# Two-block diffusion and language layer stack on one core: the spatial gate's bias moved from one-row matmuls to a VectorE addition, its product with gelu(u) moved to GpSimd

## The chip, the cores and the metric

One core of a Trainium2 chip runs the whole program. The metric is the device time of one execution in microseconds; the figure to beat is the median of the runs of the kernel before, 2892.49 us. Engines are called TensorE (PE in the rows, its weight loads PEld), VectorE (DVE), ScalarE (ACT), GpSimd (POOL) and SyncE (SP, which here only issues transfers).

## The reference, cut to what matters

The input passes through a first block of two layers (512 tokens of x and 256 tokens of a context, 1024 features, four branches of 256 features each) and then through a second block of two layers with a scan, attention and feed-forward parts. The change touches one branch of the first block only, the spatial gate:

```python
def _spatial_gate(u, v, w_sp, b_sp):
    b, n = u.shape[:2]
    nch = n // CHUNK
    u = jax.nn.gelu(u, approximate=False).reshape(b, nch, CHUNK, SGU_GROUPS, GROUP_W)
    v = jax.nn.gelu(v, approximate=False).reshape(b, nch, CHUNK, SGU_GROUPS, GROUP_W)
    sp = jnp.einsum('gpq,bmqgc->bmpgc', w_sp, v) + b_sp.T[None, None, :, :, None]
    return (u * sp).reshape(b, n, BRANCH_W)
```

CHUNK is 128, there are 4 groups of 64 features. For each chunk of 128 tokens and each group, the tokens of gelu(v) are mixed by a 128 x 128 matrix, a bias per position in the chunk is added, and the result is multiplied by gelu(u). The first layer does it for x (4 chunks) and for the context (2 chunks), the second layer for x alone. The result o_c is the fourth of the branches, and goes on, gated by silu(z), to the merge.

## The kernel before, in words

The program is one straight run of instructions. `layer` (line 569) is called for l = 0 and l = 1; l = 0 is "full" (both streams), l = 1 has x alone. All large products are in float32r with operands split into a high and a low part: `mm3` (line 236) issues three matmuls, high x high (L237), and the two mixed ones (L238, L239). `fm` (line 241) runs them over 8 tiles of features with the weights stationary, 512 (x) or 256 (context) tokens moving. `wload` (line 218) brings 1 MB of weights by one transfer of SyncE's queue into `wraw`, ScalarE casts each half to `whi` (L232), and the low part `wlo` is a subtraction (L233), the first half of the feature tiles on VectorE, the second on GpSimd. There are two buffers of each.

The stretch around the change, in program order: the gate's matrices and its bias are loaded by GpSimd's queue (L610, L612), the matrices are transposed (L615, L617); heads of the first attention branch are made (`proj_heads`), and those of the second beside what follows, piece by piece (`beside`): norms and rotations that pass between ScalarE, VectorE and GpSimd (L966 to L997). Then come the products for v (weights `wcv`, gelu at L640, token-major into `v`), the products for u (weights `wcu`, gelu at L648, feature-major into `u`), the gate itself (L651 to L662), and the Fourier branch, whose products (L679) use a third set of weights, `wbf`, loaded at L673; ScalarE copies them out (L680). Transforms over channels and tokens (L688 to L728) and the attention (`attn1`) follow.

In the gate, for each of two feature tiles j and each stream i, a bank `ps` of PSUM collects, for every chunk m and half h (64 features), an ordinary float32 product of `v` (stationary, 128 rows x 64 columns) with the transposed matrix (moving, 128 columns), and on top of it a product of a row of ones with the row of the bias (one row x 64 columns, 128 moving). VectorE multiplies the full bank by gelu(u) into the branch's tile Y(3, j) in SBUF (L661). A float32 matmul is issued as two instructions on TensorE.

A scheduler in the tile framework orders the instructions of every engine by readiness and priority from its own model and places all waits; the Fourier branch's loads (L670, L672), for instance, stand in the code behind the gate and ran long before it. On the engines, order is then fixed. `urgent` gives the weights' casts and subtractions priority between L632 and L674. After the gate `warm` (L732), a ScalarE instruction that has the exponential's table loaded, reads one element of the last Y(3, 1).

Of the kernel before, what the change touches and what calls it, by code (L numbers as in the profile page):

```python
# [27 lines left out]
# columns of the constant array cst (128 rows)  # L28
# [68 lines left out]
class Kern:  # L97
# [23 lines left out]
    def mt(self):  # L121
        """a bank for products, from the standing ones and those that the phase has lent"""
        self.turn += 1
        pool, tag = self.banks[self.turn % len(self.banks)]
        return self.tl(pool, [P, 512], F32, tag)
# [19 lines left out]
    # ---------------------------------------------------------------- set-up  # L145
# [27 lines left out]
    def setup1(self):  # L173
        """what the first normalisation does not need"""
        nc, I = self.nc, self.I
        nc.gpsimd.dma_start(self.cst[:, P:], I["cst"][:, P:CST_KEEP])
        mk = self.mk = self.tl(self.vp, [P, 2, P], F32, "mk")
        nc.gpsimd.dma_start(mk, I["cst"][:, CST_KEEP:].rearrange("p (a b) -> p a b", a=2))
        self.sink = self.tl(self.cp, [1, 8], F32, "sink")
        nc.gpsimd.dma_start(self.sink, I["sink_d"].rearrange("a b -> (a b)").unsqueeze(0))  # L180
        for gi in (1, 2):
            self.vec_load(gi, nc.gpsimd)
# [34 lines left out]
    # ---------------------------------------------------------------- helpers  # L217
# [23 lines left out]
    def fm(self, ps, w, c0, act, n, m=P, first=True, last=True):  # L241
        """feature-major: ps[m, n] (+)= W[:, c0:c0+m]^T act"""
# [5 lines left out]
    def tm(self, ps, w, c0, n, act, t0, m=P, first=True, last=True):  # L248
        """token-major: ps[m tokens, n] (+)= act^T W[:, c0:c0+n]"""
# [5 lines left out]
    def split(self, hi, lo, src, n=None, eng=None):  # L255
        """hi + lo = src exactly (hi, lo f32r)"""
# [3 lines left out]
    def rsq(self, src, scale, eps, shape, tag="rsq"):  # L260
        """1/sqrt(src*scale + eps) on a small tile"""
# [14 lines left out]
    def stats_fm(self, ssq, n, dim, tag="nrm"):  # L276
        """ssq: squares [128, n] summed over the feature tiles -> r [128, n/128] (token on the partition)"""
# [6 lines left out]
    def add_sq(self, pool, ssq, src, k, tag="sq", bufs=2):  # L284
        """ssq (+)= src^2, tile k of eight; the last added on the vector engine"""
# [14 lines left out]
    def norm_fm(self, tp, xs, n, ssq, w, bias, hi_tag, lo_tag, pool):  # L300
        """xs: 8 feature tiles [128, n], ssq: their squares summed; h = xs*r*w + bias, as hi, lo pairs. In three steps:
        the sums, the factors, the tiles"""
# [16 lines left out]
    # a norm whose factor 1/rms per token is applied after the products: the tiles are scaled by the weight and split as  # L319
    # they are finished  # L320
# [12 lines left out]
    def norm_units(self):  # L333
        """runs evacuations one unit late; the norm's factors follow behind the first and the second unit"""
# [15 lines left out]
    # ---------------------------------------------------------------- first block  # L350
    def silu_c(self):
        """columns silu(c), silu(c_ctx), padded with zeros to 32 columns per k tile"""
# [15 lines left out]
    def ada(self, l, parts):  # L368
        """nb[l][i] = (norm_w*(1+sc), sh, gt) as columns [128, 8] for i = x, ctx: the first two in part 0, the last in
        part 1; yields after every piece"""  # L370
# [5 lines left out]
        def load(m):  # L376
            """two pieces of 1024 columns: of one row tile in part 0, of two in part 1"""
# [50 lines left out]
    def layer0_norm(self, i, hcp):  # L428
        """token-major rms of x or ctx, then, in two halves of the features, feature-major f32"""
# [20 lines left out]
    def ada0(self, h, pool):  # L450
        """the first layer's norm_w*(1+sc) and sh for feature tiles 4h..4h+3; yields after every row tile"""
# [19 lines left out]
        # even and odd row tiles go to column groups of their own  # L471
# [26 lines left out]
    def proj_kv0(self, ada, st, hcp):  # L498
        """the first layer's inputs, and the keys and values of both attention branches, token-major; the second half of
        the features follows the first, so that the products start on half of the modulation"""  # L500
# [68 lines left out]
    def layer(self, l, bst, hcp):  # L569
# [36 lines left out]
        # ---- attention A: heads; SGU and fourier branches beside it  # L606
# [4 lines left out]
        bsp = self.tl(p1, [1, 512], F32, "bsp")  # L611
        nc.gpsimd.dma_start(bsp, I["b_sp"][l].rearrange("g p -> (g p)").unsqueeze(0))  # L612
# [18 lines left out]
        # ---- spatial gate and fourier branches  # L631
# [18 lines left out]
        # spatial gate  # L650
        for j in range(2):  # L651
            for i in streams:
                ps = self.mt()
                for m in range(NS[i] // P):
                    for h in range(2):
# [3 lines left out]
                                 start=True, stop=False)  # L659
                        T.matmul(o, self.ones[0:1, 0:64], bsp[0:1, g * P:(g + 1) * P], start=False, stop=True)  # L660
                V.tensor_tensor(Y(3, j)[i][0], ps[:, :NS[i]], u[i][j], ALU.mult)  # L661
                beside(2)  # L662
        # fourier mix
# [30 lines left out]
        # outputs n and N - n share their cosine and sine sums  # L694
# [35 lines left out]
        # has the exponential's table loaded ahead of the first softmax  # L730
# [6 lines left out]
        # ---- the two attentions  # L737
# [4 lines left out]
        def gates(rs, pool, tag, bufs, steps):  # L742
            """gates z of some branches, applied to them in place"""
# [36 lines left out]
        # ---- gates z  # L780
# [28 lines left out]
        # ---- merge  # L809
# [3 lines left out]
        def merged(i, d):  # L813
            """the merged tile d of stream i (four times its value), split for the output projection"""
# [43 lines left out]
        # ---- output projection and residual  # L858
# [54 lines left out]
    def proj_kv(self, l, st, gc, gx):  # L913
        """finishes the inputs of both streams; keys and values of both attention branches, token-major"""
# [27 lines left out]
    def proj_heads(self, l, br, acts, full, ap, kv):  # L942
        """q, k, v of one attention branch, token-major, rms-normed and rotated"""
# [18 lines left out]
        for half, src, nh, tts in ((0, q, 4, ntt if full else 4), (1, k, 2, ntt)):  # L962
            # rotation tables times the norm's weight
# [38 lines left out]
    def heads_T(self, br, kv, hds, tr, full, ap):  # L1002
        """feature-major exact splits of one group: q stacked [hi; lo], k twice [hi; hi] and [lo; lo]"""
# [27 lines left out]
    def attn1(self, l, hds, tr, Y, full, ap, at, fills):  # L1031
        """grouped attention over [x 512 | ctx 256] keys; br 0 full, br 1 window with sink. Scores and softmax run two
        head tiles ahead of the transposes, those one ahead of p v"""
# [5 lines left out]
        def scores(m):  # L1039
# [11 lines left out]
            # (psum column, key column, width, masks)  # L1051
# [63 lines left out]
    def normalised(self, out, po, sums, nq, pool, tag, bufs=None):  # L1115
        """out = po / sums, for two heads [64, tokens] one above the other; sums [128, tokens/128, 2]"""
# [11 lines left out]
    def run(self, gen):  # L1128
        """exhausts a generator and returns its value"""
# [6 lines left out]
    def every(self, gen, n):  # L1136
        """a generator that advances gen on every n-th step"""
        for _ in gen:
            for _ in range(n):
                yield  # L1140

    def pipeline(self, n, stages):
        """runs stage(m) for m < n; a stage with lag k and period p runs k steps late, on the last of each p items"""
# [6 lines left out]
class Kern2(Kern):  # L1150
    # ---------------------------------------------------------------- rotary tables
    def sincos(self, pool, ang, shape, sin_out, cos_out, tag):
        """sin and cos of ang (f32, any size up to about 1e6): exact reduction mod pi/2, polynomials"""
# [13 lines left out]
        # m = k mod 4  # L1167
# [15 lines left out]
        # quadrants: k = m >= 2, r = odd  # L1183
# [15 lines left out]
    def exp_acc(self, pool, x, shape, tag):  # L1199
        """x <- exp(x) to float32 accuracy, on the vector engine"""  # L1200
# [38 lines left out]
    def rope_tm(self, pool, x, nh, half, cs, sn, out, tag):  # L1239
        """x [P, 4, nh, 2*half] token-major, overwritten; out (may be x) = rotated"""  # L1240
# [12 lines left out]
    def residual(self, act, w, k0=0, scale=None, feed=None, pool=None):  # L1253
        """x += (act @ w (rows k0*128 on)) [* scale]; feeds the next norm if asked; yields after every tile"""
# [20 lines left out]
    # ---------------------------------------------------------------- even layer  # L1275
# [5 lines left out]
    def causal64(self, sc, qi):  # L1281
        """keys of the second half of the diagonal block are hidden from queries of its first half"""
# [29 lines left out]
    def even(self):  # L1312
# [11 lines left out]
        # ---- differential attention  # L1324
# [6 lines left out]
        def proj(g):  # L1331
            """q, k, v of heads 2g, 2g+1, token-major, rotated; and the first head's tiles"""
# [29 lines left out]
        def head(hd, part):  # L1362
            """feature-major exact splits: q stacked [hi; lo], k twice [hi; hi] and [lo; lo]"""
# [16 lines left out]
        def gates(chunks, pool, tmp, steps):  # L1380
            """gates z of the state space branch: twice silu"""
# [42 lines left out]
        def combine(m):  # L1424
            """e0 - lam*(sum0/sum1)*e1: the difference of the two softmaxes, times sum0"""
# [63 lines left out]
        # ---- state space branch  # L1489
# [28 lines left out]
        # dt  # L1518
# [5 lines left out]
        # z; beside it the splits of the attention branch, which goes through its half of the output projection beside the scan  # L1524
# [30 lines left out]
        def done(t):  # L1555
            """gated tile t (twice its value): squares and weighted split for the gated norm"""
# [26 lines left out]
    def softplus(self, pool, src):  # L1583
        """dt [P, 4, 16] (token on the partition) = softplus(src + dt_bias); also -dt*exp(a_log)"""
# [35 lines left out]
    def ssd(self, mp, m1, xs, bT, cT, dt, z, side, done):  # L1620
        """chunks of 128 tokens; xs, bT, cT hold twice their values; xs becomes twice the gated output"""
# [92 lines left out]
    # ---------------------------------------------------------------- feed-forward  # L1714
    def ffn(self, i, last):
# [44 lines left out]
        def weighted(d, t0, n, sq):  # L1760
            """feature tile d, tokens t0..: squares, and token-major the final norm's input times its weight"""
# [23 lines left out]
        if last:  # L1785
            # the last two feature tiles by halves of the tokens: the first half leaves beside the second's products
# [33 lines left out]
class Kern3(Kern2):  # L1820
    # ---------------------------------------------------------------- S5 matrices (from the weights alone)
    # groups g = g2*16 + o2*8 + q; partition (o2, p); unit u = g2*8 + q; chunks of 8 tokens
    def cmul(self, eng, pool, shape, are, aim, bre, bim, ore, oim, tag, conj=False):
        """(ore + i oim) = (are + i aim)(bre + i bim); with conj: oim is minus the imaginary part, aim is given negated"""
# [25 lines left out]
    def s5_coef(self, pool):  # L1850
# [37 lines left out]
        # f = (a - 1)/lam  # L1888
# [454 lines left out]
```

## Time and profile before

| | |
|---|---|
| median of three runs | 2892.49 us (2885.21, 2892.49, 2893.84) |
| span of the profiled execution, first to last instruction | 2888.1 us |
| TensorE matmuls busy | 2797.2 us, 97% |
| TensorE weight loads busy | 2306.0 us, 80% |
| VectorE / ScalarE / GpSimd busy | 1419.7 / 1001.6 / 891.6 us |
| mean granted TensorE clock | 0.982 of full speed |

The profiled execution's own time is not listed apart from the three runs; its span lies 4.4 us under their median and inside their spread. A matmul's end is modelled and overlaps the start of the next, so the spacing of starts is what one costs in a row; a granted clock of 1.00 is 2.4 GHz, 0.50 is 1.2 GHz.

### The profile page before, as it was taken

Reading aid. Unit: us, or ns where it says so; the run is one execution under the profiler, and the core shown is the slowest. Engines: PE = TensorE matmul, PEld = TensorE weight load, DVE = VectorE, ACT = ScalarE, POOL = GpSimd, SP = SyncE. Lnnn points to the kernel's source line nnn. Section 1 sums busy time; section 2 is a strip of 40 time slices with the busy share of each in tenths; the row PEclk is TensorE's granted clock in tenths of the full one; section 3 lists DMA queues with packets and bytes.
Section 4 is the critical chain, followed back from the end, with each engine's and each line's share of the span. In section 5 each row is a group of like instructions: output and inputs, shape, how many; then the busy total and the mean of one; then the engine's idle time right before and its main releaser. Section 6 shows DMA issues by size and latency. Waiting matters only on the chain.

```text
span 2888.1 us, 40028 instructions
## 1 busy us (share of the span) xinstructions
PE 2797.2 (97%) x16056; PEld 2306.0 (80%) x16056; DVE 1419.7 (49%) x2786; ACT 1001.6 (35%) x1796; POOL 891.6 (31%) x676
## 2 busy tenths in 40 slices
PE   7999999999999999999999989999999997999998
PEld 4966788888897888888988767788888865788887
DVE  5615521112346446544577787655542375655532
ACT  3325532222343552333455342332222342432222
POOL 4400153232233124333322232533332220333332
PEclk9989999999998999999999999999999998999999
DMA  6216222121222113332322221223222214233232
GB/s 241 64 43 198 79 63 74 55 73 52 96 72 69 54 52 110 117 108 88 88 81 67 52 90 43 69 83 107 93 95 95 84 45 81 81 94 108 91 99 84
DMA packets 221102, 247.99 MB, mean 86 GB/s; under 512 B 14191, under 2 KB 205268, under 8 KB 219892
## 3 DMA queue, kind: packets, MB, share of 16 engines
q1 hardware_dynamic: 218788, 240.76, 27.0%
q0 software_dynamic: 2128, 4.67, 0.8%
q8 instruction: 126, 2.06, 0.3%
q14 instruction: 60, 0.49, 0.1%
HBM read 231.28 MB, written 6.78 MB: 82 GB/s over the span
## 4 chain that ended last, share of the span: by engine, by line
PE 41%; DVE 4%; issue 4%; DMA 2%; ACT 1%; POOL 1%; SPq 0%; ACTq 0%; POOLq 0%; DVEq 0%
PE ex L237 7%; PE ex L238 7%; PE ex L239 7%; PE mm L237 5%; PE mm L238 5%; PE mm L239 5%; DVE xs L1512 1%; PE mat L2178 1%; DMA s5T<-dkk 1%; PE sg L1676 1%; DVE wlo L233 0%; PE mpo L2208 0%; DMA dcol<-in_ev_d_skip 0%; PE tp L2195 0%; DMA dk<-dk 0%
## 5 line engine op out<-in xcount | busy, mean ns | idle before, releaser
L233 POOL TENSOR_TENSOR wlo<-wraw,whi 128x1024 fp32r<-128x1024 f32 (+3 forms) x180 | 442.0, 2456 | 901.7 <-ACT whi L232 891.6
L232 ACT CAST whi<-wraw 128x1024 fp32r<-128x1024 f32 (+2 forms) x360 | 352.1, 1007 | 600.8 <-issue 205.6
L233 DVE TENSOR_TENSOR wlo<-wraw,whi 128x1024 fp32r<-128x1024 f32 (+2 forms) x180 | 236.1, 1311 | 386.1 <-ACT whi L232 385.5
L237 PE MATMUL ex<-hhi,whi 128*128 128x512 f32 x1044 | 410.8, 394 | 0.6 <-ACT whi L232 0.6
L239 PE MATMUL ex<-hhi,wlo 128*128 128x512 f32 x1044 | 408.9, 392 | 1.6 <-DVE wlo L233 1.6
L238 PE MATMUL ex<-hlo,whi 128*128 128x512 f32 x1044 | 408.6, 391 | 0.0
L237 PE MATMUL mm<-hhi,whi 128*128 128x512 f32 x708 | 282.2, 399 | 4.0 <-ACT whi L232 3.9
L238 PE MATMUL mm<-hlo,whi 128*128 128x512 f32 x708 | 279.0, 394 | 3.2 <-DVE hlo L329 2.8
L239 PE MATMUL mm<-hhi,wlo 128*128 128x512 f32 x708 | 278.8, 394 | 2.1 <-DVE wlo L233 2.0
L239 PEld LDWEIGHTS ex<-hhi,wlo 128*128 128x128 f32 x1044 | 197.0, 189 | 44.2 <-DVE wlo L233 2.5
L237 PEld LDWEIGHTS ex<-hhi,whi 128*128 128x128 f32 x1044 | 197.2, 189 | 42.1 <-ACT whi L232 1.4
L238 PEld LDWEIGHTS ex<-hlo,whi 128*128 128x128 f32 x1044 | 197.2, 189 | 39.8
L237 PEld LDWEIGHTS mm<-hhi,whi 128*128 128x128 f32 x708 | 134.0, 189 | 34.3 <-ACT whi L232 4.8
L239 PEld LDWEIGHTS mm<-hhi,wlo 128*128 128x128 f32 x708 | 133.8, 189 | 31.9 <-DVE wlo L233 3.4
L238 PEld LDWEIGHTS mm<-hlo,whi 128*128 128x128 f32 x708 | 134.0, 189 | 31.0 <-DVE hlo L329 4.1
L237 PE MATMUL mm<-whi,hhi 128*128 128x256 f32 (+1 forms) x464 | 135.3, 292 | 0.1
L239 PE MATMUL mm<-whi,hlo 128*128 128x256 f32 (+1 forms) x464 | 132.5, 286 | 1.4 <-DVE hlo L329 1.4
L238 PE MATMUL mm<-wlo,hhi 128*128 128x256 f32 (+1 forms) x464 | 132.5, 286 | 0.6 <-DVE wlo L233 0.6
L237 PE MATMUL ex<-fhi,whi 128*128 128x512 f32 (+1 forms) x308 | 111.9, 363 | 0.0
L239 PE MATMUL ex<-fhi,wlo 128*128 128x512 f32 (+1 forms) x308 | 111.6, 362 | 0.0
L238 PE MATMUL ex<-flo,whi 128*128 128x512 f32 (+1 forms) x308 | 111.6, 362 | 0.0
L233 POOL TENSOR_TENSOR wblo<-wbraw,wbhi 128x256 fp32r<-128x256 f32 x32 | 26.9, 839 | 235.2 <-ACT wbhi L232 221.5
(822 smaller groups left out, 6098.0 us busy)
## 6 DMA issues: line engine op xcount, KB each, us to landing
wraw<-in_w_merge SPq DMA_DIRECT2D x32, 1024.0 KB
wraw<-in_ev_w_in SPq DMA_DIRECT2D x22, 1024.0 KB
wraw<-in_ffn_gate SPq DMA_DIRECT2D x22, 1024.0 KB
wraw<-in_ffn_up SPq DMA_DIRECT2D x22, 1024.0 KB
wraw<-in_w_in SPq DMA_DIRECT2D x20, 1024.0 KB
wraw<-in_ffn_down SPq DMA_DIRECT2D x17, 1024.0 KB
wraw<-in_w_ada SPq DMA_DIRECT2D x16, 1024.0 KB
wbraw<-in_w_br SPq DMA_DIRECT2D x32, 256.0 KB
```

The costliest lines, as they stand in the source:

```text
L232: self.S.copy(hi[:, a:b], raw[:, a:b])
L233: e.tensor_tensor(lo[:, a:b], raw[:, a:b], hi[:, a:b].bitcast(F32), ALU.subtract)
L237: self.T.matmul(ps, lh, rh, start=first, stop=False)
L238: self.T.matmul(ps, lh, rl, start=False, stop=False)
L239: self.T.matmul(ps, ll, rh, start=False, stop=last)
L1512: V.scalar_tensor_tensor(o, cv[:, tap:tap + 512], cw[:, tap * 12 + t:tap * 12 + t + 1], o, ALU.mult, ALU.add)
L1676: T.matmul(sg[:, j * P:(j + 1) * P], mk, self.c("uincl"), start=True, stop=True)
L2178: T.matmul(sc[:, :n], qT[:, qi * P:(qi + 1) * P], kT[:, :n], start=True, stop=False)
```

## The change: what it does, and the diff

The bias is loaded as a tile of 128 partitions: row 64h + c holds, for j = 0, 1, the 128 biases of group 2j + h, the same for all 64 c. Two transfers of GpSimd's queue per layer, each repeating 256 numbers into 64 partitions, take the place of one. The one-row matmuls go; each remaining product opens and closes its own sum. VectorE adds the bias as it moves the bank to Y(3, j), reading the bias tile with a repeat over the chunks, and GpSimd multiplies Y(3, j) by gelu(u) in place. Elsewhere the diff only removes comments.

```diff
-        bsp = self.tl(p1, [1, 512], F32, "bsp")
-        nc.gpsimd.dma_start(bsp, I["b_sp"][l].rearrange("g p -> (g p)").unsqueeze(0))
+        bsp = self.tl(p1, [P, 2, P], F32, "bsp")
+        for h in range(2):
+            nc.gpsimd.dma_start(bsp[64 * h:64 * h + 64], I["b_sp"][l].rearrange("(j h) p -> h j p", h=2)[h].unsqueeze(0)
+                                .to_broadcast([64, 2, P]))
...
                         T.matmul(o, v[:, 4 * i + m, g * 64:g * 64 + 64], wspT[:, g * P:(g + 1) * P],
-                                 start=True, stop=False)
-                        T.matmul(o, self.ones[0:1, 0:64], bsp[0:1, g * P:(g + 1) * P], start=False, stop=True)
-                V.tensor_tensor(Y(3, j)[i][0], ps[:, :NS[i]], u[i][j], ALU.mult)
+                                 start=True, stop=True)
+                y = Y(3, j)[i][0]
+                V.tensor_tensor(y.rearrange("p (m q) -> p m q", q=P), ps[:, :NS[i]].rearrange("p (m q) -> p m q", q=P),
+                                bsp[:, j].unsqueeze(1).to_broadcast([P, NS[i] // P, P]), ALU.add)
+                G.tensor_tensor(y, y, u[i][j], ALU.mult)
                 beside(2)
```

## Rows read from the trace of the kernel before

**Rows 1.** The page: its head, and the engines' busy time.

```profile
span 2888.1 us, 40028 instructions
...
PE 2797.2 (97%) x16056; PEld 2306.0 (80%) x16056; DVE 1419.7 (49%) x2786; ACT 1001.6 (35%) x1796; POOL 891.6 (31%) x676
```

**Rows 2.** Instructions of the one-row matmuls' line; duration ns min/median/max, first and last start.

```profile
L660 PE MATMUL ex<-bsp,ones x56: 267/416/471, 148.2 to 921.2; 1*64 1x128 f32 x56
...
L660 PE MATMUL mm<-bsp,ones x24: 416/442/471, 153.9 to 167.7; 1*64 1x128 f32 x24
```

**Rows 3.** Busy us by stretch of layer 0's gate; PEclk is the granted clock.

```profile
147.80:153.90 6.10, 6.10 (x35) 3.20 (x34) 0.18 (x1) 1.67 (x2) 0.00 (x0) 1.00 0.00 0
153.90:173.00 19.10, 19.10 (x63) 8.88 (x62) 1.63 (x3) 0.00 (x0) 0.00 (x0) 0.50 0.00 1
173.00:177.50 4.50, 4.50 (x12) 3.51 (x12) 0.42 (x1) 0.20 (x1) 0.00 (x0) 0.50 0.00 0
```

**Rows 4.** Timeline of TensorE, layer 0, gate and Fourier products: start us, us.

```profile
147.80 0.43 PE L658 MATMUL ex<-wspT,sguv 128*64 128x128 f32 x2
148.16 0.43 PE L660 MATMUL ex<-bsp,ones 1*64 1x128 f32 x2
...
173.03 0.80 PE L237 MATMUL ex<-hhi,whi 128*128 128x512 f32 x1
...
178.09 0.40 PE L237 MATMUL ex<-hhi,whi 128*128 128x512 f32 x1
...
180.85 0.28 PE L237 MATMUL ex<-chi,whi 128*128 128x256 f32 x1
```

**Rows 5.** Timeline of TensorE, layer 1, the Fourier products behind the gate.

```profile
921.55 0.80 PE L237 MATMUL ex<-hhi,whi 128*128 128x512 f32 x1
...
922.57 0.63 PE L239 MATMUL ex<-hhi,wlo 128*128 128x512 f32 x1
...
925.45 0.40 PE L237 MATMUL ex<-hhi,whi 128*128 128x512 f32 x1
```

**Rows 6.** Timeline of TensorE in layer 0's attention.

```profile
236.40 1.53 PE L1107 MATMUL mm<-pt,hkv 128*64 128x128 f32 x24
237.86 0.39 PE L1071 MATMUL at<-tk,tq 128*128 128x256 f32 x1
...
257.43 0.43 PE L1107 MATMUL mm<-pt,hkv 128*64 128x128 f32 x2
257.79 0.44 PE L1093 MATMUL tp<-cst,e 128*128 128x128 f32 x2
```

**Rows 7.** Timeline of ScalarE, VectorE and GpSimd before and beside layer 1's gate.

```profile
907.74 0.38 ACT L640 ACTIVATE sguv<-ex 128x256 f32<-128x256 f32 x1
...
883.82 1.42 DVE L997 TENSOR_TENSOR hq<-hq,hrs 128x256 f32<-128x256 f32 x4
...
907.68 3.58 DVE L997 TENSOR_TENSOR hq<-hq,hrs 128x256 f32<-128x256 f32 x4
...
915.89 1.22 DVE L233 TENSOR_TENSOR wlo<-wraw,whi 128x1024 fp32r<-128x1024 f32 x1
...
919.37 0.68 DVE L661 TENSOR_TENSOR y<-ex,sguu 128x512 f32<-128x512 f32 x1
...
907.91 2.40 POOL L233 TENSOR_TENSOR wlo<-wraw,whi 128x1024 fp32r<-128x1024 f32 x1 [0.47 <-ACT whi L232]
```

**Rows 8.** Timeline of VectorE, ScalarE and GpSimd around layer 0's gate.

```profile
141.24 1.22 DVE L233 TENSOR_TENSOR wlo<-wraw,whi 128x1024 fp32r<-128x1024 f32 x1
...
173.66 0.20 ACT L732 ACTIVATE warm<-xc 1x1 f32<-1x1 f32 x1 [24.08 <-DVE xc L661]
...
198.83 0.60 POOL L702 DMA_DIRECT2D fc<-in_dft  x1 [61.14 <-PE ex L720]
```

**Rows 9.** GpSimd's in-place multiplication of a branch by its gate z.

```profile
L759 POOL TENSOR_TENSOR x<-x,mt x8: 1289/1292/1297, 355.6 to 415.3; 128x512 f32<-128x512 f32 x8
```

**Rows 10.** GpSimd's issue of the bias transfer, both layers.

```profile
L612 POOL DMA_DIRECT2D bsp<-in_b_sp x2: 518/524/530, 79.4 to 825.7; - x2
```

## The prediction, made before the changed kernel ran

> **What bounds the kernel.** I read the page first. TensorE is busy 97% of a span of 2888.1 us, and no other engine passes half [rows 1]: what shortens TensorE's own run of work, and is not given back in a wait, shortens the kernel. Then the one-row matmuls' line: 56 + 24 = 80 instructions [rows 2], which is 40 matmuls, 24 in layer 0 (two feature tiles, six chunks, two halves) and 16 in layer 1, in two instructions each. As many products of v stay. Then the stretches of layer 0's gate by time: TensorE's granted clock is 1.00 (2.4 GHz) for the first 6.1 us, 0.50 (1.2 GHz) for the next 19.1 us, and still 0.50 in 4.5 us of the Fourier products behind it [rows 3]. So the gate takes 25.2 us of TensorE, from 147.80 to 173.03 [rows 4], and slows what follows. Its 96 instructions cost 180 ns each while the clock is full: 0.36 us from the pair of line 658 to the pair of line 660 [rows 4].
>
> The last view settles what the products cost alone. In the attention, line 1107 has the same shape (128 rows, 64 columns, 128 moving, float32, the two column halves taking turns every two instructions). 24 of them in a row take 1.46 us, from 236.40 to 237.86, so 61 ns each; a lone pair between products of another shape takes 0.36 us, from 257.43 to 257.79, again 180 ns each [rows 6]. It is the change of shape every two instructions that is dear, and the one-row matmuls cause it. Removing them removes their time and two thirds of their neighbours'.
>
> **Part 1, TensorE in layer 0.** 48 instructions stay: 48 x 61 ns = 2.9 us, with 0.2 us for coming in from another shape (a lone pair's 0.36 less 2 x 61 ns) 3.1 us, so the Fourier products start at 150.9 and not at 173.03: 22.1 us. Do they find their weights? The last subtraction for them on VectorE ends at 141.24 + 1.22 = 142.5 [rows 8], 8 us before. In that stretch nothing else is late. The clock: the gate had 6.1 us at full clock before it fell [rows 3], and now ends after 3.1, so I take it that it does not fall. Then the first 12 Fourier products, 5.06 us from 173.03 to 178.09, cost what the next 12 do, 2.76 us [rows 4]: 2.3 us more. Layer 0 gives 24.4 us.
>
> **Part 2, TensorE in layer 1.** Here the gate hides something. TensorE would be through the gate early: the last chunk of v is ready at 908.1 [rows 7], and 20 instructions behind it take 1.2 us, so 909.3. But VectorE, which is in a closed run of work for the second heads, subtracts the first half of the Fourier weights only at 915.89, until 917.11 [rows 7]. That instruction waits for nothing of the gate, so it stays there. The third Fourier product, the first to read that half, started at 922.57 [rows 5] and can now start at 917.1: 5.5 us. TensorE comes to it after a pause of 8 us; I let it be at 1.2 GHz for about as long as it was at 921.55, to 925.45 [rows 5], which lasts 0.7 us longer in product time than what remained of it before. I take 4.5 us. From below: if the additions are put ahead of that subtraction on VectorE it is up to 2 x 0.68 us [rows 7] later, and GpSimd's multiplications can hold it up: the same four instructions of line 997 took 3.58 us beside a subtraction of GpSimd (907.91, 2.40 us) and 1.42 us at 883.82 [rows 7], 2.2 us more, about one GpSimd instruction. That leaves 1 to 2 us. From above: with the subtraction early, 921.55 - 909.3 = 12.2 us, and 1.8 us more for the first 9 products at full clock (3.90 us against 9 x 0.23) [rows 4, 5]: 14 us.
>
> On those held-up instructions, the Trainium skill (SBUF — State Buffer, Who interferes with whom) says that a VectorE instruction with two inputs in SBUF and a GpSimd instruction that reads SBUF exclude each other for a whole instruction. The trace agrees (3.58 against 1.42 us); by it layer 1 would give some 2 us instead of 4.5 if both multiplications ran before 917.
>
> **Part 3, the evacuation.** VectorE's instruction stays in number and shape, PSUM and one SBUF operand in; it was 0.68 us for 512 tokens [rows 7]. No row has the repeated bias operand. Between the same 0.68 and twice that, it costs nothing, since the banks of the gate are not the next that the Fourier products take. New on GpSimd are four multiplications in layer 0 and two in layer 1. The in-place one of line 759 takes 1.29 us [rows 9]; all six are under 8 us. In layer 0 GpSimd is idle for 61 us up to 198.83 [rows 8], and nothing queues behind them. In layer 1 its weight subtraction starts at 907.91 [rows 7]; I take the multiplications to come behind it. Who waits for the product? First `warm` on ScalarE, with the copies of the Fourier products behind it. It ran at 173.66, when VectorE had finished [rows 8]; now it waits for GpSimd too: the last products end at 150.9, addition and queued multiplications bring that to 153.5 or so, and the first copy is due when 24 Fourier products are through, 5.5 us after 150.9. Cover: 3 us. If it fails, copies come late, but the transforms that read them stand further behind. Nothing.
>
> **Part 4, the transfers.** One more transfer in each layer on GpSimd's queue, 0.52 us of issue each [rows 10], in front of heads and a weight subtraction. They start some 70 us ahead of the gate. Between 0 and 1 us each, if many more packets are slower to issue; I take 0.5 in all.
>
> **Sum.** 24.4 + 4.5 - 0.5 = 28.4 us. The span would be 2859.7. Against the median, 4.4 us above the span, 2892.5 - 28.4 = **2864 us**. A measurement of this kernel can tell about 0.3%, 8.7 us, from no change.
>
> **Rivals.** (a) *The remaining products stay at 180 ns*, the shape change not being the reason. For it: the gate has only been seen at this price. Against: line 1107 [rows 6]. Layer 0 would be 48 x 180 ns = 8.6 us, or 10.4 if the clock falls again after 6.1 us (34 instructions, then 14 at the 303 ns that 19.1 us for 63 of them give [rows 3]): 14.8 to 16.6 us saved, perhaps 2.3 with the clock. Layer 1 stays at 4.5, bound by 917.1. 19 to 23 us: 2869 to 2873. The Trainium skill (TensorE: Matmul & The Clock Gate, Part 3) has a rule on this side: a weight load overlaps matmuls in flight only when the row group differs, and the products left use all rows. By it they would not overlap; the 61 ns of line 1107, whose row groups do not differ either, speak against it. Chance 0.11.
>
> (b) *VectorE's order frees the weights early in layer 1*: the scheduler, with other times, moves the subtraction up. Then 24.4 + 14 = 38 us: 2854. Against: nothing ahead of it depends on the gate. 0.10.
>
> (c) *The time is given back*: work behind the gate in layer 0 is bound by something that does not move. Against: TensorE is the busy engine there too. Within 8.7 us: 2884 to 2901. 0.05.
>
> (d) *Slower*: the scheduler reorders TensorE's work in the attention, so that its runs of one shape are cut up. Place: line 1107, 61 ns in a long run and 180 ns in a pair [rows 6]. Price: 0.12 us for each instruction that loses its run. It decides when the loss passes the 28 us saved; to be slower by 8.7 us it takes 37 / 0.12 = 308 instructions. For it: the order comes from a model that sees the change. Against: little changes ahead of the attention but a shift in time. With 340 so cut, 2905. 0.03.
>
> **Numbers.** The forecast has 0.71, (a) 0.11, (b) 0.10, (c) 0.05, (d) 0.03. Faster: the first three, 0.92; same 0.05; slower 0.03. The range takes in (a) up to 2873 and (b) down to 2854 with some 3 us for the spread of runs (2885 to 2894): 2851 to 2876.
>
> **What would show it.** Right: line 658 in layer 0 as one run of 48 instructions in about 3 us, the Fourier products at about 151 at a clock of 1.00 from the start; in layer 1 a TensorE pause of 7 to 9 us that ends with VectorE's `wlo`. Wrong: 180 ns between products of line 658 (rival a); no pause in layer 1 (b); new idle time of TensorE between 170 and 300, or shorter runs of line 1107 (c, d).

## The result and the profile after

The changed kernel took 2862.48 us (median of 4 runs, 2858.03 to 2865.51) against 2890.65 us for the kernel before in runs beside it (4 runs, 2885.21 to 2893.84). The ratio is 0.9897, with a 95% interval of 0.9874 to 0.9920: faster by 1.0%, 28.2 us between the medians. In the changed file the product of the gate stands at line 660, VectorE's addition at 663, GpSimd's multiplication at 665; the transforms of 688 and 706 are now 692 and 710, `warm` is 736 and line 997 is 1001.

The page of the changed kernel, its head and the engines' busy time, answers to [rows 1]:

```profile
span 2856.1 us, 39868 instructions
...
PE 2758.6 (97%) x15976; PEld 2287.8 (80%) x15976; DVE 1418.5 (50%) x2786; ACT 1000.1 (35%) x1796; POOL 897.6 (31%) x684
```

The span is 32.0 us shorter. TensorE has 80 instructions less and 38.6 us less busy time, GpSimd eight instructions more (six multiplications and two transfers), VectorE the same number.

TensorE's timeline in layer 0 (start us, us), where the gate is now one run of 16 + 24 + 8 = 48 instructions, to set against [rows 4]:

```profile
148.64 1.09 PE L660 MATMUL ex<-wspT,sguv 128*64 128x128 f32 x16
149.57 1.48 PE L660 MATMUL mm<-wspT,sguv 128*64 128x128 f32 x24
150.88 0.61 PE L660 MATMUL ex<-wspT,sguv 128*64 128x128 f32 x8
151.41 0.50 PE L237 MATMUL ex<-hhi,whi 128*128 128x512 f32 x1
...
154.29 0.39 PE L237 MATMUL ex<-hhi,whi 128*128 128x512 f32 x1
```

The gate goes from 148.64 to 151.41, 2.8 us where it was 25.2. The first 12 Fourier products take 2.88 us, to 154.29, where they took 5.06 [rows 4]. The stretches of time say why (as in [rows 3]; behind the length stand busy us and instructions of PE, PEld, DVE, ACT and POOL, then the granted clock, the share of the DMA engines and GB/s):

```profile
148.60:151.40 2.80, 2.80 (x49) 2.60 (x48) 1.33 (x3) 1.67 (x2) 0.78 (x1) 1.00 0.00 0
151.40:160.00 8.60, 8.60 (x51) 7.60 (x50) 0.72 (x2) 0.79 (x2) 3.14 (x4) 1.00 0.01 2
...
884.80:891.50 6.70, 1.29 (x4) 0.50 (x2) 6.36 (x19) 1.82 (x2) 2.42 (x1) 0.50 0.00 0
```

In layer 0 the granted clock is 1.00 (2.4 GHz) through the gate and behind it. In layer 1 it is 0.50 (1.2 GHz) from 884.8 to 891.5, a stretch in which TensorE is busy for 1.29 of 6.70 us. TensorE's timeline there (the bracket is the idle time before an instruction and what ended it) answers to [rows 5]:

```profile
878.86 0.66 PE L660 MATMUL ex<-wspT,sguv 128*64 128x128 f32 x8
880.37 0.44 PE L660 MATMUL ex<-wspT,sguv 128*64 128x128 f32 x4 [0.85 <-ACT sguv L642]
882.53 2.40 PE L660 MATMUL ex<-wspT,sguv 128*64 128x128 f32 x20 [1.72 <-ACT sguv L642]
884.86 0.80 PE L237 MATMUL ex<-hhi,whi 128*128 128x512 f32 x1
...
891.52 0.79 PE L239 MATMUL ex<-hhi,wlo 128*128 128x512 f32 x1 [5.43 <-DVE wlo L233]
...
904.01 1.00 PE L692 MATMUL tp<-wf,c 128*128 128x64 f32 x8
```

TensorE waits three times: twice for ScalarE's gelu of v inside the gate, then 5.43 us for VectorE's `wlo`. VectorE's timeline shows what that subtraction stands behind, to set against [rows 7]:

```profile
882.04 3.59 DVE L1001 TENSOR_TENSOR hq<-hq,hrs 128x256 f32<-128x256 f32 x4
...
890.25 1.22 DVE L233 TENSOR_TENSOR wlo<-wraw,whi 128x1024 fp32r<-128x1024 f32 x1
...
893.73 1.28 DVE L663 TENSOR_TENSOR y<-ex,bsp 128x512 f32<-128x512 f32 x2
```

The weights' half is ready at 891.5, and the gate's additions come 2.2 us behind it. What follows them on the two other engines:

```profile
894.49 2.53 POOL L665 TENSOR_TENSOR y<-y,sguu 128x512 f32<-128x512 f32 x2 [6.66 <-DVE y L663]
```

```profile
897.05 0.20 ACT L736 ACTIVATE warm<-y 1x1 f32<-1x1 f32 x1 [10.42 <-POOL y L665]
898.77 0.59 ACT L684 COPY fT<-ex 128x512 f32<-128x512 f32 x1 [1.51 <-PE ex L239]
```

`warm` ends 1.5 us before the first copy of the Fourier products is due. So it holds up nothing yet, but little is left.

The gain, from one starting point to the next: layer 0's gate begins 0.84 us later than before (an early wait for the first weights' transfer, 7.4 against 6.6 us, makes most of it); the Fourier products begin 21.6 us sooner (173.03 to 151.41), the transforms behind them 23.8 us sooner (192.01 to 168.18), layer 1's gate 25.6 us sooner (904.50 to 878.86), and its first transforms 30.3 us sooner (934.32 to 904.01).

### The profile page after: what moved, and what is told of

Read it like the earlier page. It is cut to its first block, busy times and chain, and to the rows that moved or that the text cites. A ratio compares the mean times of both kernels' runs of the same rounds, so it can differ in the third digit from the quotient of the medians.

```text
span 2856.1 us, 39868 instructions
## 1 busy us (share of the span) xinstructions
PE 2758.6 (97%) x15976; PEld 2287.8 (80%) x15976; DVE 1418.5 (50%) x2786; ACT 1000.1 (35%) x1796; POOL 897.6 (31%) x684
## 3 DMA queue, kind: packets, MB, share of 16 engines
q1 hardware_dynamic: 218788, 240.76, 27.3%
## 4 chain that ended last, share of the span: by engine, by line
PE 42%; DVE 4%; issue 4%; DMA 2%; ACT 1%; POOL 1%; SPq 0%; ACTq 0%; POOLq 0%; DVEq 0%
PE ex L238 7%; PE ex L237 7%; PE ex L239 7%; PE mm L237 5%; PE mm L238 5%; PE mm L239 5%; DVE xs L1516 1%; PE mat L2182 1%; DMA dk<-dk 1%; PE sg L1680 1%; DMA s5T<-dkk 1%; DVE wlo L233 0%; PE mpo L2212 0%; DMA dcol<-in_ev_d_skip 0%; PE tp L2199 0%
```

## The experiments

In the edits below "before" and "changed" say which kernel is edited. The kernel before took 2889.84 us (13 runs) beside experiments 1 to 4, 2894.73 (11) beside 6, 7, the first run of 8 and 9, and 2894.80 (7) beside 5, the second run of 8 and 10; all ratios are against those. Three dots in an edit or in rows mark a cut.

**1. GpSimd's product alone.** The change's other half without the matmul's: before, with the evacuation split in two.

```diff
-                V.tensor_tensor(Y(3, j)[i][0], ps[:, :NS[i]], u[i][j], ALU.mult)
+                y = Y(3, j)[i][0]
+                V.tensor_copy(y, ps[:, :NS[i]])
+                G.tensor_tensor(y, y, u[i][j], ALU.mult)
```

> The kernel before with its one-row matmuls, VectorE only copying the bank out and GpSimd multiplying by gelu(u): half of the change alone. I expect no difference, span 2888 within 5 us: six GpSimd instructions, under 8 us, in stretches where nothing queues behind them. If the product on GpSimd costs something by itself, it shows here as a later start of the Fourier products or of their copies.

2890.36 us, ratio 1.0004 (0.9992 to 1.0016): no difference that these runs can tell. Its layer 0 gate took 27.0 us, from 149.09 to 176.13.

**2. The product back on VectorE.** Changed, one word.

```diff
-                G.tensor_tensor(y, y, u[i][j], ALU.mult)
+                V.tensor_tensor(y, y, u[i][j], ALU.mult)
```

> The changed kernel with the product with gelu(u) back on VectorE, behind the addition: GpSimd gets nothing new. If the time comes from TensorE alone, as I hold, this is the changed kernel again: span 2856 within 4 us, layer 0's gate 2.8 us, layer 1's pause ended by the same VectorE subtraction. If GpSimd's part matters (a product that holds up the ScalarE instruction behind it, or a VectorE that is too full for both), it differs by over 4 us, to either side.

2858.57 us, ratio 0.9887 (0.9872 to 0.9901), not to be told from the change's. `warm` ran 2.2 us behind the first Fourier product (155.12 and 152.90) where it was 3.2 us behind in the changed kernel, and in layer 1 the third Fourier product waited 5.50 us for VectorE's `wlo`, as with the change. The gain comes from what is done to the one-row matmuls; which engine multiplies makes no difference that these runs can tell.

**3. The same matmuls with 128 rows.** Before, with as many instructions, in the same order on TensorE; the bias is row 0 of a zeroed tile, so the sum is the same.

```diff
-        bsp = self.tl(p1, [1, 512], F32, "bsp")
+        bsp = self.tl(p1, [P, 512], F32, "bsp")
+        G.memset(bsp, 0.0)
...
-                        T.matmul(o, self.ones[0:1, 0:64], bsp[0:1, g * P:(g + 1) * P], start=False, stop=True)
+                        T.matmul(o, self.ones[:, 0:64], bsp[:, g * P:(g + 1) * P], start=False, stop=True)
```

> The kernel before with as many matmuls, but the bias product made in the shape of its neighbours: 128 rows of ones against a tile that holds the bias in row 0 and zeros below. If it is the change of shape that is dear, the 96 instructions of layer 0's gate take 96 x 58 ns = 5.6 us instead of 25.2, the clock stays at 1.00 there, and layer 1 gains the same 4.7 us as the changed kernel, since VectorE's subtraction ends its wait: 22 + 5 - 1 = 26 us, span about 2862. If it is the number of matmuls, the gate stays at about 25 us and the span at 2888.

2859.78 us, ratio 0.9889 (0.9872 to 0.9905). TensorE's timeline:

```profile
148.45 0.45 PE L659 MATMUL ex<-wspT,sguv 128*64 128x128 f32 x4
148.72 0.40 PE L661 MATMUL ex<-bsp,ones 128*64 128x128 f32 x4
...
153.89 0.50 PE L237 MATMUL ex<-hhi,whi 128*128 128x512 f32 x1
```

The 96 instructions take 5.4 us. So it was not their number that cost 25.2 us, but that every second pair had another number of rows.

**4. One-row matmuls, grouped.** Before, with one bias matmul per half and bank ahead of all products of the bank, so that the shape changes twice per bank.

```diff
+                n = NS[i]
+                for h in range(2):
+                    g = 2 * j + h
+                    T.matmul(ps[64 * h:64 * h + 64, :n].rearrange("c (m q) -> c m q", q=P), self.ones[0:1, 0:64],
+                             bsp[0:1, g * P:(g + 1) * P].unsqueeze(1).to_broadcast([1, n // P, P]), start=True, stop=False)
...
-                                 start=True, stop=False)
-                        T.matmul(o, self.ones[0:1, 0:64], bsp[0:1, g * P:(g + 1) * P], start=False, stop=True)
...
+                                 wspT[:, g * P:(g + 1) * P], start=False, stop=(m == n // P - 1))
```

(The 128 biases of a group are read again for each chunk, so 8 one-row matmuls in layer 0 cover the columns that 24 covered before.)

> The kernel before with one-row matmuls kept, but one per half bank, ahead of the products, its bias row repeated over the chunks: 8 one-row matmuls in layer 0 and 4 in layer 1 instead of 24 and 16, and two changes of shape per bank instead of one every two instructions. If the change of shape is dear: per bank of 512 about 4 x 0.22 + 16 x 0.058 + 2 x 0.24 = 2.3 us, of 256 about 1.4, so layer 0's gate 7 to 8 us, span about 2864. If an instruction beside one-row matmuls costs 180 ns wherever it stands, the gate takes about 12 us and falls to half clock.

2863.73 us, ratio 0.9905 (0.9890 to 0.9919). TensorE's timeline:

```profile
147.91 1.07 PE L657 MATMUL ex<-bsp,ones 1*64 1x512 f32 x4
148.91 1.09 PE L662 MATMUL ex<-wspT,sguv 128*64 128x128 f32 x16
...
154.29 0.50 PE L237 MATMUL ex<-hhi,whi 128*128 128x512 f32 x1
```

The gate takes 6.4 us with one-row matmuls in it, over as many columns. What is dear is the alternation, not the one row.

**5. How many rows.** As in 3, with 32 and with 64 rows in place of 128.

```diff
-        bsp = self.tl(p1, [P, 512], F32, "bsp")
+        bsp = self.tl(p1, [64, 512], F32, "bsp")
...
-                        T.matmul(o, self.ones[:, 0:64], bsp[:, g * P:(g + 1) * P], start=False, stop=True)
+                        T.matmul(o, self.ones[0:64, 0:64], bsp[:, g * P:(g + 1) * P], start=False, stop=True)
```

> The kernel before with the bias product on 32 rows (31 of them zero) between products of 128 rows. If any change in the number of rows is dear, this is the kernel before: pairs 0.36 us apart at full clock, layer 0's gate some 25 us, span about 2888. If it is the single row, the gate falls toward the 5.4 us of the version with 128 rows.

> The same with 64 rows. If any change in the number of rows is dear, 25 us and 2888 again; if the cost shrinks as the shapes come closer, between 5.4 and 25 us.

One run each: 2877.93 us with 32 rows, 2872.13 with 64. TensorE's timeline with 64 rows, the first pairs and the last:

```profile
149.00 0.43 PE L659 MATMUL ex<-wspT,sguv 128*64 128x128 f32 x2
149.36 0.43 PE L661 MATMUL ex<-bsp,ones 64*64 64x128 f32 x2
...
165.96 0.43 PE L661 MATMUL ex<-bsp,ones 64*64 64x128 f32 x2
166.32 0.50 PE L237 MATMUL ex<-hhi,whi 128*128 128x512 f32 x1
```

The gate takes 17.3 us, all pairs 0.36 us apart, and the clock stays whole, as the stretch shows:

```profile
149.00:166.30 17.30, 17.30 (x97) 9.09 (x96) 1.81 (x3) 1.67 (x2) 0.00 (x0) 1.00 0.00 1
```

With 32 rows the pairs are 0.36 us apart too until the clock falls, 9.4 us into the gate:

```profile
148.00:157.70 9.70, 9.70 (x57) 5.18 (x55) 1.12 (x2) 1.67 (x2) 0.00 (x0) 1.00 0.01 2
157.70:171.20 13.50, 13.50 (x47) 6.21 (x45) 0.69 (x1) 0.00 (x0) 0.00 (x0) 0.51 0.00 0
```

It takes 22.8 us (148.41 to 171.19). So the price of a pair at full clock is the same with 1, 32 and 64 rows, while the time to the fall of the clock is not. Layer 1's gates, one of each kernel, go the same way: the clock falls 3.6 us in with one row (experiment 6, 879.57 to 883.17), 10.1 us in with 32 (901.99 to 912.07), and not in the 11.6 us with 64.

What happens within a pair is seen in the weight loads. Those of the 64-row kernel:

```profile
149.00 0.19 PEld L659 LDWEIGHTS ex<-wspT,sguv 128*64 128x64 f32 x2
149.36 0.19 PEld L661 LDWEIGHTS ex<-bsp,ones 64*64 64x64 f32 x2 [0.17 <-issue]
149.72 0.19 PEld L659 LDWEIGHTS ex<-wspT,sguv 128*64 128x64 f32 x2 [0.17 <-issue]
```

and those of the 128-row kernel of experiment 3, whose program order is the same:

```profile
148.44 0.20 PEld L659 LDWEIGHTS ex<-wspT,sguv 128*64 128x64 f32 x4
148.61 0.26 PEld L661 LDWEIGHTS ex<-bsp,ones 128*64 128x64 f32 x4
```

With other rows the engine of the loads stands idle for 0.17 us before each pair of them, and nothing that the profile shows holds it. With the same rows four loads go in 0.20 us: the product of the second column half starts about 0.01 us behind that of the first, though the first half's bias matmuls stand ahead of it in the program. (The order that is fixed in the program is thus not the order of starts on TensorE.) The halves run side by side, each a new instruction every 0.11 us (148.61 to 148.72). Equal rows thus give two things: no gap, and two halves at once.

It need not be the rows that differ. The lone pair of [rows 6] in the kernel before has 64 columns between instructions of 128 columns, all with 128 rows, and its loads show the same gap on both sides:

```profile
257.43 0.19 PEld L1107 LDWEIGHTS mm<-pt,hkv 128*64 128x64 f32 x2 [0.17 <-issue]
257.79 0.20 PEld L1093 LDWEIGHTS tp<-cst,e 128*128 128x128 f32 x2 [0.17 <-issue]
```

No experiment varies the columns by themselves.

**6. The change in layer 0 alone.** Changed, with the old gate in layer 1.

```diff
-                                 start=True, stop=True)
+                                 start=True, stop=full)
+                        if not full:
+                            T.matmul(o, self.ones[0:1, 0:64], bs1[0:1, g * P:(g + 1) * P], start=False, stop=True)
                 y = Y(3, j)[i][0]
+                if not full:
+                    V.tensor_tensor(y, ps[:, :NS[i]], u[i][j], ALU.mult)
+                    beside(2)
+                    continue
```

(In layer 1 the bias row `bs1` is loaded by one transfer, and VectorE multiplies at once, as before.)

> The change in layer 0, layer 1's gate as in the kernel before (its one-row matmuls and its product on VectorE). If the two gates add up as their stretches read, layer 0 alone gives 22.5 us for the gate, 2.3 for the clock behind it, so 24 to 26 us against the kernel before, and layer 1's 4 to 5 us are missing against the changed kernel: span about 2861. If layer 1's waits made its gate free, the span is 2856 as changed.

2864.78 us (6 runs), ratio 0.9905 (0.9889 to 0.9921). Layer 1's gate again took 17.2 us, 879.57 to 896.73, though VectorE's `wlo` was ready at 892.1.

**7. The changed kernel again,** beside 6, 8 and 9.

> The changed kernel once more, on the chip of the last three, to compare with: span 2856 within 4 us.

2860.11 us, ratio 0.9887 (0.9869 to 0.9905). The median is 4.7 us below that with layer 0 alone, but the intervals of the two ratios overlap.

**8. The Fourier weights' first half on GpSimd in layer 1.** Changed; the subtraction that TensorE waits for moves to the engine that does the second half. No other instruction of any engine changes its place. Run twice.

```diff
-            for a, b, e in ((0, h, self.V), (h, kt, self.G)):
+            for a, b, e in ((0, h, lo_eng or self.V), (h, kt, self.G)):
...
-        wbf = self.win(l, 1536)
+        wbf = self.win(l, 1536, lo_eng=None if full else G)
```

> The changed kernel with one instruction moved in layer 1: the first half of the Fourier weights' subtraction goes from VectorE to GpSimd, ahead of the second half. If VectorE's place for it is what ends TensorE's pause, the pause of 5.4 us goes: the third Fourier product starts within 1 us of the second, the clock is low for a shorter time, and the Fourier products end some 6 us sooner against the changed kernel. Span about 2850, ratio to the changed kernel 0.998. If something else is late there too, the pause stays at 3 us or more.

> The version with the Fourier weights on GpSimd once more, beside the swap and for a second sample against the changed kernel: 2855 us within 4, ratio 0.987 to 0.989 to the kernel before.

2855.73 us (ratio 0.9879, 0.9860 to 0.9897) and 2857.60 us (0.9874, 0.9856 to 0.9892). TensorE's timeline of the first run:

```profile
882.97 2.40 PE L660 MATMUL ex<-wspT,sguv 128*64 128x128 f32 x20 [1.73 <-ACT sguv L642]
...
886.32 0.63 PE L239 MATMUL ex<-hhi,wlo 128*128 128x512 f32 x1
...
901.42 1.13 PE L710 MATMUL tp<-bd,fT 128*128 128x256 f32 x4 [1.80 <-ACT bd L696]
```

The 5.43 us wait is gone, but the transforms of line 710 now wait 1.80 us for ScalarE, whose timeline has

```profile
898.63 0.20 ACT L736 ACTIVATE warm<-y 1x1 f32<-1x1 f32 x1 [11.57 <-POOL y L665]
...
900.63 0.73 ACT L696 COPY bd<-tp 64x256 f32<-64x256 f32 x2
```

`warm` still waits for GpSimd's product and, through it, for VectorE's addition, and the copies queue behind it. The cover of 1.5 us is used up, and the edit itself takes part of it: `warm` runs 19.3 us behind the gate's start (898.63 - 879.30) where it ran 18.2 us behind (897.05 - 878.86), although VectorE has an instruction of 1.22 us less to do. Its four instructions of line 1001 now stand beside three subtractions of GpSimd and take longer than the 3.59 us above:

```profile
884.61 5.76 DVE L1001 TENSOR_TENSOR hq<-hq,hrs 128x256 f32<-128x256 f32 x4
```

**9. Heads kept out of the gate's gelus.** As 8, and in layer 1 no head work is called between the chunks of v.

```diff
-            beside(1)
+            beside(1 if full else 0)
```

> As the one with the Fourier weights on GpSimd, and in layer 1 no pieces of the second heads are put between the products for v, so that ScalarE's gelus are not queued behind the heads' squares. If these gelus make TensorE wait 0.85 and 1.72 us within the gate, both go: some 2.5 us less again, span about 2848. If the heads come due later because of it, the time comes back in front of the attention and the span is 2850 or more.

2859.58 us, ratio 0.9883 (0.9866 to 0.9901), and TensorE's two waits for the gelus were still 0.85 and 1.73 us. This tested nothing: the scheduler gave every engine the same instructions in the same order as in 8, so the gelus stayed where they were, and these runs are a third sample of 8.

**10. The last gelu ahead of the casts.** As 8, and in layer 1 v's gelu gets a high priority, which puts the last of them ahead of the two weight casts in ScalarE's order and changes nothing else.

```diff
-            S.activation(v[:, tt, :], ps[:, :256], AF.Gelu)
+            with (nullcontext() if full else self.tc.high_priority()): S.activation(v[:, tt, :], ps[:, :256], AF.Gelu)
```

> The version with the Fourier weights on GpSimd, and in layer 1 the last gelu of v ahead of the casts of those weights on ScalarE (one swap). TensorE's pause of 1.7 us within the gate goes, the weights come 0.4 us later; the third Fourier product starts about 1 us sooner after the gate's start. In the total this is under what five rounds can tell: within 0.1% of that version.

2859.62 us, ratio 0.9879 (0.9865 to 0.9894): no gain over 8. TensorE's timeline:

```profile
881.27 1.59 PE L660 MATMUL ex<-wspT,sguv 128*64 128x128 f32 x24 [0.85 <-ACT sguv L642]
...
895.63 1.00 PE L692 MATMUL tp<-wf,c 128*128 128x64 f32 x8
901.91 2.07 PE L710 MATMUL tp<-bd,fT 128*128 128x256 f32 x4 [4.84 <-ACT bd L696]
```

The second wait is gone and the Fourier products end 1.7 us sooner than in the second run of 8 (895.63 and 897.31, both with the gate's start at 879.76), but line 710 starts at the same time (901.91 and 901.90): the wait for ScalarE grew from 3.15 to 4.84 us.

From the start of layer 1's gate to the first instruction of line 710 (706 before, other lines in experiments 5 and 6) the traces give:

| kernel | us |
|---|---|
| before; layer 0 alone (6) | 32.1; 32.0 |
| changed; again (7) | 27.4; 27.3 |
| experiment 8, both runs; 9; 10 | 22.1, 22.1; 22.1; 22.1 |
| experiment 5, 64 rows (line 707) | 25.4 |

All four profiles with the early weights stop at the same 22.1 us; by their waits it is `warm` and the copies behind it that set this. The early weights are thus worth 5.2 us at line 710. Some of it is given back: the instruction of line 1076 that starts 90.4 and 90.0 us behind the gate in the two profiles of the changed kernel starts 86.1 to 86.9 us behind it in these four. In the times it is 3.1 us between means (13 runs of 8 and 9 together 2858.0, eight of the changed kernel 2861.2), where single runs of either spread by 8 to 9 us: a likely small gain, not a shown one. A version in which `warm` reads something that is ready sooner was not tried.

The last row of the table shows a second price of the waits. With 64 rows, layer 1's gate takes 11.6 us, not 6.0, but TensorE has almost no wait in it or behind it, and the clock stays whole:

```profile
894.00:905.60 11.60, 11.60 (x65) 6.06 (x64) 10.70 (x32) 6.88 (x10) 6.79 (x8) 1.00 0.00 1
905.60:915.00 9.40, 9.06 (x40) 7.17 (x39) 4.59 (x10) 0.79 (x2) 0.00 (x0) 1.00 0.66 224
```

The third Fourier product, held by VectorE's `wlo`, comes 12.6 us behind the gate's start there and 12.7 us in the changed kernel; from it to the end of the Fourier products it is 10.6 us there and 12.5 us here, where the clock is down at first. So this one gate, the slower by itself, ends 2.0 us ahead at the transforms.

## Why the prediction was right

**Size and sign.** The forecast was a gain of 28.4 us; the medians differ by 28.2, the spans by 32.0. The interval of the ratio reaches from 23 to 36 us, so that the two agree within 0.2 us is luck. The two profiles of the same changed kernel have spans of 2856.1 and 2861.6 us and agree within 0.5 us up to 1025 us, so some 5 us of a span are the later part's own spread, and the predicted 2859.7 lies between them. In the profile shown, TensorE's instructions stand 30.4 us sooner from layer 1's transforms to 1480 us of the kernel before; all of that but 1.8 us is in the parts below, less the 0.84 us by which the first gate begins later.

**Part 1, layer 0.** The step from [rows 6] held: 58 ns for each of the 48 instructions (2.77 / 48) where line 1107 gave 61. The gate gave 22.5 us for 22.1, the Fourier products behind it 2.2 for 2.3, the clock not falling. The reason given for the clock, that the gate would be over before the 6.1 us at which it had fallen, was weak: the same gate lost it after 3.6 us in experiment 1, and the 64-row gate kept it for 17.3 us. Rival (a), products that stay at 180 ns, fell with TensorE's timeline of layer 0.

The price of one change of shape was taken as a single number; the experiments take it apart. Of the 25.2 us, by differences between kernels, 7.9 us are the fall of the clock (25.2 less 17.3 with 64 rows), 11.9 us the change of rows at full clock (17.3 less 5.4 with 128 rows), 2.6 us the number of matmuls (5.4 less 2.8), and 2.8 us stay. The 11.9 us can be split by an estimate: 96 instructions at 0.11 us, one half at a time and without gaps, are 10.5 us, so some 5 us come from the halves no longer running side by side and some 7 us from the gaps.

On that, the Trainium skill (TensorE: Matmul & The Clock Gate, Part 3) has the rule weighed in the prediction, that a weight load overlaps matmuls in flight only if its row group differs. The loads of experiment 3 go against it, as line 1107 did: four of them, all with the same 128 rows, go within 0.20 us, the later ones while products are in flight. The 0.17 us of idle time before each pair of loads with other rows, which are among those 128, decides nothing about it.

**Part 2, layer 1.** 4.7 us (32.1 less 27.4 in the table) for 4.5. The medians of experiments 6 and 7 differ by as much, which agrees but, with intervals that overlap, shows nothing by itself. What bounds it was named rightly: VectorE's `wlo`, in its place in the run for the heads. Moved by the 25.6 us that layer 1's gate begins sooner, its steps come out one by one: v's last chunk forecast at 908.1 - 25.6 = 882.5, and those products start at 882.53; the weights' half at 917.1 - 25.6 = 891.5, and the third Fourier product starts at 891.52. The lower clock behind it was to take back 0.7 us: the third product came 5.41 us sooner after the gate's start, of which 4.7 remain. Only the pause was not the 7 to 9 us forecast: the last 20 products took 2.4 us at 1.2 GHz where 1.2 us had been put, and two Fourier products another 1.2 us, which leaves 5.43 us of it. Both lie in the same wait and change no sum.

Rival (b), the weights ready early, did not come by itself; experiment 8 made it happen. The Fourier products end 25.2 us after the gate's start in the changed kernel (904.01 - 878.86), 18.9 and 17.5 us in the two runs of experiment 8, and 15.9 us in experiment 10, where a wait for a gelu is gone as well: 6.3, 7.6 and 9.3 us less, for the rival's 14 - 4.5 = 9.5. What reached line 710 was 5.2 us. The step that failed, in the rival alone, is that nothing would be late next: `warm` is.

**Part 3, the evacuation and GpSimd.** The addition with the repeated bias operand takes 0.68 to 0.69 us for 512 tokens, the lower of the two bounds. The products take 1.28 us, as [rows 9] had for line 759, and cost nothing (experiments 1 and 2). The additions came behind `wlo` and the multiplications behind both, so the feared hold-up did not touch the weights. The cover for `warm` in layer 0 was named rightly: forecast to run at 153.5, it ran at 154.57, and the first copy was due at 157.21.

The four instructions of line 1001 took 3.59 us, beside a subtraction of GpSimd. That is the hold-up of [rows 7] again and agrees with the Trainium skill (SBUF — State Buffer, Who interferes with whom), as weighed in the prediction: 3.59 us beside GpSimd, 1.42 us without [rows 7].

**Part 4.** The second bias transfer doubles GpSimd's issue (0.52 to 1.24 us), and the wait for the gate's weights beside it in layer 0 grew from 0.75 to 0.85 us: 0.1 us where 0.5 was allowed.

**Not forecast.** Between layer 0's transforms (23.8 us sooner) and layer 1's gate (25.6) lie 1.8 us that no part of the change has a price for. In the kernel before the granted clock was down for part of the way, 0.93 in the stretch

```profile
810.00:835.00 25.00, 22.92 (x154) 20.87 (x153) 19.20 (x50) 10.40 (x19) 7.12 (x9) 0.93 0.17 57
```

and the stretch that answers to it in the changed kernel had it whole:

```profile
786.00:811.00 25.00, 22.91 (x167) 20.96 (x166) 20.34 (x52) 11.35 (x21) 7.79 (x10) 1.00 0.20 61
```

25 us times 0.07 is 1.8 us. It is not one run's accident: in the same stretch of work the clock is 0.93 in all three profiles of kernels whose gate in layer 0 lost its clock (before, experiment 1, 32 rows) and 1.00 in the other eleven. How a gate 600 us earlier would bring that about stays open. Rivals (c) and (d) left no trace: the time saved in layer 0 was still there at layer 1's gate, and outside the gates TensorE has the same matmuls in the same order before and after.

## What to carry to other kernels

Where TensorE alternates between shapes with different numbers of rows (and, by the one pair above, of columns), count the changes, not the matmuls: each pair of float32 instructions cost 0.36 us here against 0.12 in a run of one shape, and the clock fell on top. Grouping by shape (6.4 us), or padding the small operand with zeros to the same rows (5.4 us), gave nearly all that removing the matmuls gave (2.8 us), which helps where no other engine can take the addition. And before a late operand is moved forward, ask what comes next: here, close behind the wait of 5.43 us, lay that of a one-element instruction with a queue of copies behind it, and moving the subtraction held up VectorE on the way to it.

## What was not expected of the hardware

- The price of a pair, 0.36 us at full clock, is the same with 1, 32 and 64 rows beside 128, but the time for which the clock stays whole is not: it fell 6.1 us into layer 0's gate with 1 row (3.6 us in experiment 1), 9.4 us in with 32, and not at all in 17.3 us with 64 (one profile each for 32 and 64). TensorE counts as busy all the way in each of them.
- Two column halves of one shape run side by side even past a matmul that stands between them in the program, where all have the same 128 rows (experiment 3).
